# Gate and up in seven block products instead of eight, in a two-layer trunk on one core

## The chip, the cores and the metric

The kernel runs on one core of a Trainium2 chip, in one launch. The metric is the device time of that core in microseconds (us), the median over several executions of the program. Five engines work side by side, each through its own queue of instructions and in order: TensorE (PE, with its weight loads shown apart as PEld), VectorE (DVE), ScalarE (ACT), GpSimd (POOL) and SyncE (SP), which here issues most DMAs. An instruction that needs another engine's result waits at the head of its queue, and what stands behind it waits too.

## The reference

Two layers over 512 tokens of 1024 features. Each layer is a mixer and a feed-forward network (FFN), each inside a sandwich of norms:

```
for layer in range(2):
    x = x + rmsnorm(mixer(rmsnorm(x, mix_pre_g)), mix_post_g)
    x = x + rmsnorm(swiglu(rmsnorm(x, ffn_pre_g)), ffn_post_g)

def swiglu(h, w_gate, w_up, w_down):     # [512, 1024], two of [1024, 2816], [2816, 1024]
    return (silu(h @ w_gate) * (h @ w_up)) @ w_down
```

The mixer of layer 0 is forgetting attention (8 heads) beside causal pooling, that of layer 1 a gated linear recurrence. All is float32. The change concerns `h @ w_gate` and `h @ w_up`, and what makes and uses their operands.

## The kernel before

**Products.** A float32 operand a is held as two parts, ah and al, and a product is ah·bh + ah·bl + al·bh, three matmuls into the same bank of PSUM (`mm3`, L124 to L126). Weights come in units of 128 x 1024: SP loads a unit into one of 3 `raw` tiles (L142), ScalarE casts it to the high part (`whi`, L143), and VectorE subtracts to get the low part (`wlo`). VectorE's instructions are issued through a helper, so most of them bear its line, L89. `whi` and `wlo` have 4 buffers each. `unit()` hands out the next unit and issues the loads and splits of the two behind it, with high priority.

**Order.** Instructions are put into the program in the order of the code, each on its engine's queue; a scheduler that knows priorities may move some forward. Work for TensorE that needs results of other engines is put back by hand: `later(delay, fn)` queues it behind so many us of matmuls as counted by `tick`, and `need(...)` calls what is left of it up to the token blocks named.

**The end of a mixer.** `TokenMajor` makes the output projection of each block of 128 tokens; `Finish` then makes, per token block, the post-norm (two Squares on ScalarE L573, a product with the gain on VectorE, a power on GpSimd L553), the residual sum (`xres`), the next pre-norm (Square L590, power, `tmp<-xres,small,gain`), the transposes on TensorE (L610), and the split of the transposed activations into hTh (ScalarE, L613) and hTl (VectorE). The steps of one block follow each other from engine to engine. Blocks 2 and 3 come last, while the FFN already begins.

**The FFN.** 22 tiles of 128 gate columns and 22 of up columns, each the product of a unit with all 512 tokens over 8 slices of k: 24 matmuls. The first four tiles run in halves of 256 columns (`split_proj`), first over token blocks 0 and 1 in all four, then over 2 and 3, so that TensorE works while blocks 2 and 3 are still being normalised. The other 40 tiles are matmuls of 512 columns (`proj`) that read hTh and hTl as four pieces of 128. A pair's gate tile goes through Silu (L706), VectorE multiplies with the up tile (`tmp<-tmp,ps`), ScalarE casts the high part (`gT`, L709) and GpSimd subtracts the low part (L710). The down projection takes 22 units: 16 for all blocks, then the last 6 block by block, each block followed by its `Finish`.

**The start.** The first projection takes 8 steps k (`vs`, values and gates), each with one load of x and weights (L216 to L219) and matmuls of 264 and 256 columns. A load of constants (`in_sh`, L241) and three loads of weights follow; the constants' casts on VectorE (`idb`, `maskb`) stand in the queue between steps of this projection.

Of the kernel before, what the change touches and what calls it, by code (L numbers as in the profile page):

```python
# [15 lines left out]
P = 128  # L16
D = 1024
# [4 lines left out]
FT = FF // P  # L22
EPS = 1e-6
# [3 lines left out]
# columns of the packed per-partition constants and parameters  # L27
# [23 lines left out]
# shape constants: identity | causal mask | zeros, upper triangle with the diagonal, ones  # L51
# [7 lines left out]
def tile_trunk(ctx: ExitStack, tc: tile.TileContext, cst_d, sh_d, xw_d, x_d, gains_d, pw_d, w_d, out_d):  # L59
    """Every float32 product a.b is carried as ah.bh + ah.bl + al.bh on float32r,  # L60
    where ah holds the top 12 bits of a and al = a - ah the rest, exactly."""
# [17 lines left out]
    class Recorded:  # L79
        """an engine that remembers the last instruction given to it"""  # L80
# [21 lines left out]
    # work for the tensor engine that is queued behind `delay` us of other work of it,  # L102
    # while what it needs is being made
# [19 lines left out]
    def mm3(out, ah, al, bh, bl, start, stop, us=0.65):  # L123
        nc.tensor.matmul(out, lhsT=ah, rhs=bh, start=start, stop=False)  # L124
        nc.tensor.matmul(out, lhsT=ah, rhs=bl, start=False, stop=False)  # L125
        nc.tensor.matmul(out, lhsT=al, rhs=bh, start=False, stop=stop)  # L126
        tick(us)

# [4 lines left out]
    NU = w_d.shape[0]  # L133
# [5 lines left out]
    def split_weights(src, n, hi, lo):  # L139
        raw = pw.tile([P, D], F32, name="raw", tag="raw", bufs=3)  # L140
        with tc.high_priority():
            nc.sync.dma_start(out=raw[:, :n], in_=src)  # L142
            nc.scalar.copy(out=hi, in_=raw[:, :n])  # L143
            vec.tensor_sub(out=lo, in0=raw[:, :n], in1=f32(hi))

    def prefetch(n):
        while state["loaded"] < min(NU, state["used"] + n):
            hi, lo = place.get(state["loaded"], whl)()
            split_weights(w_d[state["loaded"]], D, hi, lo)
            ready.append((hi, lo))  # L150
            state["loaded"] += 1

# [27 lines left out]
    # the tensor engine's clock rises while the first loads are under way  # L180
# [9 lines left out]
    def log1p(out, e, u, d):  # L190
        """out = log(1 + e) for 0 <= e <= 1, with what the rounding of 1 + e takes off; u and d are scratch."""
# [7 lines left out]
    # ================= layer 0 mixer =================  # L199
# [4 lines left out]
    # values and forget gates, k outermost, on x*g; the row scale is applied on the way out.  # L204
    # columns: even heads, gates | odd heads
# [4 lines left out]
    for k in range(KT):  # L210
        xw = pw.tile([P, T + 520], F32, name="raw", tag="raw", bufs=3)
# [36 lines left out]
    # row scale of the first norm  # L248
# [41 lines left out]
    # -8 softplus(-lam)  # L290
# [4 lines left out]
    # c = cumsum(log f), as rows 32*b + 4*h + r for every b and r, by a product with the triangle  # L295
# [10 lines left out]
    def gates():  # L306
# [591 lines left out]
```

## Time and profile before

| | us |
|---|---|
| median of 3 runs | 1098.68 (1098.46 to 1099.26) |
| the profiled execution, first to last instruction | 1097.0 |
| TensorE busy in it | 1079.5 (98%) |
| VectorE busy | 485.1 (44%) |
| ScalarE busy | 421.3 (38%) |
| GpSimd busy | 139.7 (13%) |
| gate and up, layer 0 (189.32 to 437.10) | 247.8 |
| gate and up, layer 1 (721.65 to 969.51) | 247.9 |

The profile is of one execution, and its times count from the first instruction. "Busy" is the time in which at least one instruction of the engine ran. Matmuls overlap: the duration of one is longer than the distance between two starts, and what a matmul costs is read from the starts.

### The profile page before, as it was taken

How to read it: one execution, taken by the hardware profiler on the slowest of the kernel's cores; microseconds unless marked ns; L12 is line 12 of the kernel's file. 1: busy time of each engine (PE TensorE's matmuls, PEld its weight loads, DVE VectorE, ACT ScalarE, POOL GpSimd, SP SyncE). 2: the span in 40 equal slices, each digit the busy share in tenths (PEclk: the TensorE clock that was granted, in tenths of full speed). 3: DMA queues.
4: the chain of work that ended last, by engine and by line, in shares of the span. 5: the costliest groups of instructions: out<-in, count | busy, mean ns of one | idle time of the engine just before them, and what ended most of it. 6: DMA issues, size and time to landing. Idle time of an engine off the chain costs nothing.

```text
span 1097.0 us, 12987 instructions
## 1 busy us (share of the span) xinstructions
PE 1079.5 (98%) x5166; PEld 893.5 (81%) x5166; DVE 485.1 (44%) x665; ACT 421.3 (38%) x659; POOL 139.7 (13%) x140
## 2 busy tenths in 40 slices
PE   8999999999999999999999999999999999999997
PEld 7878787988888888888898887898888888888885
DVE  4899856522222222224348598543222222222323
ACT  6767634422222222114235984433222222221211
POOL 0020201111111111000003104101111111110000
PEclk9999999999999999999999999999999999999999
DMA  8644343322222222226113223313222222223401
GB/s 287 179 112 106 97 155 114 115 95 90 90 93 95 96 96 96 96 96 193 57 39 116 96 86 106 116 40 130 89 92 94 96 96 96 96 81 111 135 24 72
DMA packets 33292, 114.37 MB, mean 104 GB/s; under 512 B 4048, under 2 KB 4048, under 8 KB 33232
## 3 DMA queue, kind: packets, MB, share of 16 engines
q1 hardware_dynamic: 32656, 111.45, 31.1%
q10 hardware_dynamic: 576, 2.10, 0.5%
q8 instruction: 40, 0.66, 0.2%
q14 instruction: 20, 0.16, 0.0%
HBM read 107.24 MB, written 2.10 MB: 100 GB/s over the span
## 4 chain that ended last, share of the span: by engine, by line
PE 83%; DVE 8%; ACT 3%; issue 2%; DMA 2%; POOL 0%; SPq 0%; DVEq 0%; POOLq 0%; ACTq 0%
PE ps L125 27%; PE ps L124 27%; PE ps L126 27%; DVE wlo L89 2%; DVE tmp L89 2%; DVE cr L89 2%; DVE th L89 1%; ACT whi L143 1%; PE ps L610 1%; DMA tmp<-in_sh 1%; PE ps L475 1%; PE ps L495 1%; ACT th L774 1%; PE ps L447 0%; DMA raw<-in_xw 0%
## 5 line engine op out<-in xcount | busy, mean ns | idle before, releaser
L124 PE MATMUL ps<-hTh,whi 128*128 128x512 f32 (+1 forms) x1024 | 382.8, 375 | 0.2 <-DVE vs L89 0.2
L125 PE MATMUL ps<-hTl,whi 128*128 128x512 f32 (+1 forms) x1024 | 382.4, 374 | 0.0
L126 PE MATMUL ps<-hTh,wlo 128*128 128x512 f32 (+1 forms) x1024 | 382.4, 374 | 0.0
L143 ACT CAST whi<-raw 128x1024 fp32r<-128x1024 f32 x160 | 167.6, 1048 | 471.5 <-issue 176.2
L89 DVE TENSOR_TENSOR wlo<-raw,whi 128x1024 fp32r<-128x1024 f32 (+1 forms) x168 | 204.3, 1216 | 321.5 <-ACT whi L143 315.8
L126 PEld LDWEIGHTS ps<-hTh,wlo 128*128 128x128 f32 x1024 | 192.9, 188 | 36.6
L125 PEld LDWEIGHTS ps<-hTl,whi 128*128 128x128 f32 x1024 | 192.9, 188 | 36.3 <-issue 0.2
L124 PEld LDWEIGHTS ps<-hTh,whi 128*128 128x128 f32 x1024 | 192.5, 188 | 36.6 <-PE ps L126 0.4
L710 POOL TENSOR_TENSOR gT<-tmp,gT 128x512 fp32r<-128x512 f32 x44 | 78.4, 1781 | 407.1 <-ACT gT L709 407.1
L126 PE MATMUL ps<-whi,gT 128*128 128x512 f32 x256 | 99.6, 389 | 0.0
L124 PE MATMUL ps<-whi,gT 128*128 128x512 f32 x256 | 99.6, 389 | 0.0
L125 PE MATMUL ps<-wlo,gT 128*128 128x512 f32 x256 | 99.6, 389 | 0.0
L89 DVE TENSOR_TENSOR tmp<-tmp,ps 128x512 f32<-128x512 f32 x44 | 30.3, 688 | 144.0 <-PE ps L126 142.6
L553 POOL TENSOR_TENSOR small<-small,nhalf 128x1 f32<-128x1 f32 x28 | 15.4, 551 | 331.0 <-DVE small L89 328.4
L126 PEld LDWEIGHTS ps<-whi,gT 128*128 128x128 f32 x256 | 48.1, 188 | 10.1
L125 PEld LDWEIGHTS ps<-wlo,gT 128*128 128x128 f32 x256 | 48.1, 188 | 10.0
L124 PEld LDWEIGHTS ps<-whi,gT 128*128 128x128 f32 x256 | 48.1, 188 | 10.0
L89 DVE TENSOR_TENSOR tmp<-ps,gain 128x512 f32<-128x512 f32 x32 | 21.9, 690 | 55.5 <-ACT junk L573 55.4
L573 ACT ACTIVATE junk<-ps 128x512 bf16<-128x512 f32 x32 | 19.0, 596 | 62.0 <-PE ps L126 61.7
L124 PE MATMUL ps<-gT 128*128 128x512 f32 x96 | 37.5, 391 | 0.0
L126 PE MATMUL ps<-gT 128*128 128x512 f32 x96 | 37.4, 389 | 0.0
L125 PE MATMUL ps<-gT 128*128 128x512 f32 x96 | 37.4, 389 | 0.0
(179 smaller groups left out, 1108.3 us busy)
## 6 DMA issues: line engine op xcount, KB each, us to landing
raw<-in_w SPq DMA_DIRECT2D x180, 512.0 KB, 3.5
gain<-in_gains SPq DMA_DIRECT2D x7, 512.0 KB, 3.5
raw<-in_xw SPq DMA_DIRECT2D x6, 516.0 KB, 6.3
big<-in_x ACTq DMA_DIRECT2D x4, 512.0 KB, 6.9
big<-big SPq DMA_DIRECT2D x16, 128.0 KB, 2.6
xres<-in_x SPq DMA_DIRECT2D x4, 512.0 KB, 4.7
out_dram<-xres SPq DMA_DIRECT2D x3, 512.0 KB, 2.6
big<-tmp SPq DMA_DIRECT2D x8, 128.0 KB, 3.1
```

The lines of the kernel that those rows point to most:

```text
L89: self.last = fn(*a, **k)
L124: nc.tensor.matmul(out, lhsT=ah, rhs=bh, start=start, stop=False)
L125: nc.tensor.matmul(out, lhsT=ah, rhs=bl, start=False, stop=False)
L126: nc.tensor.matmul(out, lhsT=al, rhs=bh, start=False, stop=stop)
L143: nc.scalar.copy(out=hi, in_=raw[:, :n])
L475: nc.tensor.transpose(tp[:, b * P:(b + 1) * P], pr[i][:, j * P:(j + 1) * P], ident)
L495: nc.tensor.matmul(acc[:, dst], lhsT=v, rhs=parts[g][q][:, src], start=j == 0 and q == 0, stop=j == 3 and q == 1)
L553: nc.gpsimd.tensor_tensor(out=r, in0=ms, in1=nhalf[:, :1], op=ALU.pow)
L573: nc.scalar.activation(out=junk[:, cs], in_=acc, func=AF.Square, scale=1.0 / 32, accum_out=ss[:, hf:hf + 1])
L610: nc.tensor.transpose(tp[:, b * P:(b + 1) * P], h[:, k * P:(k + 1) * P], ident)
L710: nc.gpsimd.tensor_sub(out=v[:, 1], in0=g, in1=f32(v[:, 0]))
L774: tanhs.append(nc.scalar.activation(out=th[m], in_=ra[m], func=AF.Tanh, scale=coef[:, m:m + 1]))
```

## The change

**Blocks.** In gate and up the product h·W is cut into 2 x 2 blocks: h by its halves of tokens (blocks 0, 1 and blocks 2, 3) and of k, and W, for each pair j of gate and up tiles (256 columns each), by its halves of k and of columns. Seven block products replace eight, by Strassen's scheme in Winograd's form. There are 11 pairs j, and each of the seven products is 24 matmuls of 256 columns. The sums of activations that it needs (S1 to S4, beside the plain A11, A12 and A22) are made once per layer, on VectorE, when token blocks 2 and 3 are transposed (`Blocks.put`); they lie in hTh, hTl and two more tiles, `up`. The sums of weights (`raw<-raw`) are made for each j on VectorE before the split, and the sums of products (`y`, and `z`, `c` in `hx`) on VectorE after the matmuls. VectorE's helper now has line L100, the casts of weights L158, the transposes L743.

**The first five pairs.** A11 and A12 need blocks 0 and 1 alone. For j = 0 to 4 (LEAD) these two products run ahead, before the need for blocks 2 and 3, and their two weight quarters are loaded a second time for the sums. From j = 5 all seven products of a j come together, in the order A11, S1, S2, A12, S3, S4, A22.

**Down.** It stays 22 units with 512-column matmuls. Its activations are kept in float32 (`g`), and `part()` splits them on ScalarE and VectorE up to two units ahead of their use, into the places of hTh, hTl and `up`; GpSimd's subtractions are gone.

**Else.** There are 6 `raw` tiles instead of 3; the loads of weights in front of down's last steps go 8 units ahead instead of 10; units are laid out in another order in memory.

```diff
+LEAD = 5
+RAW = 6
+    def gate_recipes(first):
+        for j in range(LEAD):
+            recipes.append(lambda j=j: load(j, 0))
+            recipes.append(lambda j=j: load(j, 3))
+        for j in range(NP):
...
+            def q5(j=j, st=st):
+                if j < LEAD:
+                    p1(j, st)
+                st["12"] = load(j, 1)
+                add_to(st["v"], st["12"], vec)
+                return st["v"]
...
+            recipes.extend([q5, p6, p7, lambda st=st: st["22"], q4] if j < LEAD
+                           else [p1, q5, p6, p2, p7, lambda st=st: st["22"], q4])
+    class Blocks:
+        def put(self, i, tps):
...
+            def split(f, src):
+                hi, lo = (view(a)[:, :, cs] for a in slot(f))
+                nc.scalar.copy(out=hi, in_=src)
+                vec.tensor_sub(out=lo, in0=src, in1=f32(hi))
...
+            if i < 2:
+                for f, x, src in ((A11, x11, tv[0]), (A12, x12, tv[1])):
+                    split(f, src)
+                    nc.scalar.copy(out=x, in_=src)
+                return
+            ta, tb = tmp(), tmp()
+            x22, s1, s2, s3 = view(ta[:, :T]), view(ta[:, T:]), view(tb[:, :T]), view(tb[:, T:])
+            nc.scalar.copy(out=x22, in_=tv[1])
+            vec.tensor_sub(out=s1, in0=tv[0], in1=x22)
+            split(S1, s1)
+            vec.tensor_sub(out=s2, in0=s1, in1=x11)
+            split(S2, s2)
+            vec.tensor_sub(out=s3, in0=x11, in1=tv[0])
+            split(S3, s3)
+            vec.tensor_add(out=s1, in0=s2, in1=x12)
+            split(S4, s1)
+            split(A22, x22)
-        pre = split_proj(4)
-        for m in range(FT):
...
-            nc.gpsimd.tensor_sub(out=v[:, 1], in0=g, in1=f32(v[:, 0]))
+        def gate_product(bank, w, f, more=False):
+            for g in range(2):
+                for k in range(4):
...
+                    mm3(bank[:, g * 256:g * 256 + 256], wh[:, cs], wl[:, cs], fh[:, ts], fl[:, ts],
+                        not more and g == 0 and k == 0, g == 1 and k == 3, 0.356, more)
...
+        need(0, 1)
+        for j in range(LEAD):
+            led.append(first(j))
+            second(j, led[j][0])
+        need(2, 3)
+        for j in range(NP):
+            b1, y = led[j] if j < LEAD else first(j)
+            z, c = hx[:, j % 2, :T], hx[:, j % 2, T:]
+            b3 = ps()
+            gate_product(b3, unit(), S1)
+            b2 = ps()
+            gate_product(b2, unit(), S2)
+            vec.tensor_add(out=y, in0=b2, in1=y)
+            vec.tensor_sub(out=z, in0=b3, in1=y)
+            if j >= LEAD:
+                second(j, b1)
+            b4 = ps()
+            gate_product(b4, unit(), S3)
+            vec.tensor_sub(out=c, in0=z, in1=b4)
+            gated(j, 3, c, c[:, :256])
+            b5 = ps()
+            gate_product(b5, unit(), S4)
+            vec.tensor_add(out=z, in0=b5, in1=z)
+            gated(j, 2, z, z[:, :256])
+            gate_product(b4, unit(), A22, True)
+            vec.tensor_add(out=y, in0=b4, in1=y)
+            gated(j, 1, y, y[:, :256])
+        def part(k, ahead=2):
+            while len(parts) < min(FT, k + 1 + ahead):
...
+                nc.scalar.copy(out=hi, in_=src)
+                vec.tensor_sub(out=lo, in0=src, in1=f32(hi))
-        prefetch(tail + 4)
+        prefetch(TAIL + 2)
```

**Three places in the order of the instructions.** First VectorE, at the norm of blocks 2 and 3 at the end of layer 0's mixer. `xres<-tmp,small,xres` is the residual sum, of block 2 in one instruction and of block 3 in two, `tmp<-xres,small,gain` the normalised rows. Before:

```order
L89 SCALAR_TENSOR_TENSOR xres<-tmp,small,xres 128x1024
L89 TENSOR_SCALAR small<-small 128x1
L89 TENSOR_TENSOR tmp<-ps,gain 128x512
L89 SCALAR_TENSOR_TENSOR tmp<-xres,small,gain 128x512 x2
L89 TENSOR_TENSOR tmp<-ps,gain 128x512
L89 SCALAR_TENSOR_TENSOR small<-small 128x1
L89 SCALAR_TENSOR_TENSOR xres<-tmp,small,xres 128x512 x2
L89 TENSOR_TENSOR hTl<-ps,hTh 128x512
L89 SCALAR_TENSOR_TENSOR small<-small 128x1
L89 SCALAR_TENSOR_TENSOR tmp<-xres,small,gain 128x512 x2
```

The same place afterwards:

```order
L100 SCALAR_TENSOR_TENSOR xres<-tmp,small,xres 128x1024
L100 TENSOR_SCALAR small<-small 128x1
L100 TENSOR_TENSOR tmp<-ps,gain 128x512
L100 SCALAR_TENSOR_TENSOR tmp<-xres,small,gain 128x512
L100 TENSOR_TENSOR wlo<-raw,whi 128x1024
L100 SCALAR_TENSOR_TENSOR tmp<-xres,small,gain 128x512
L100 TENSOR_TENSOR tmp<-ps,gain 128x512
L100 SCALAR_TENSOR_TENSOR small<-small 128x1
L100 SCALAR_TENSOR_TENSOR xres<-tmp,small,xres 128x512 x2
L100 TENSOR_TENSOR wlo<-raw,whi 128x1024 x2
L100 SCALAR_TENSOR_TENSOR small<-small 128x1
L100 SCALAR_TENSOR_TENSOR tmp<-xres,small,gain 128x512 x2
```

Three splits of 1024 now stand between the normalised rows of block 2 and those of block 3. One subtraction of 512 for hTl no longer stands there.

On TensorE the transposes of block 3 (two groups of four, the first of each with its wait) stand in the products of the first units. Before:

```order
L124 MATMUL ps<-hTh,whi 128x256
L125 MATMUL ps<-hTl,whi 128x256
L126 MATMUL ps<-hTh,wlo 128x256
L610 MATMUL ps<-ident,tmp 128x128 [waits DVE_49]
L610 MATMUL ps<-ident,tmp 128x128 x3
L610 MATMUL ps<-ident,tmp 128x128 [waits DVE_49]
L610 MATMUL ps<-ident,tmp 128x128 x3
L124 MATMUL ps<-hTh,whi 128x256
```

and afterwards:

```order
L743 MATMUL ps<-ident,tmp 128x128 [waits DVE_49]
L743 MATMUL ps<-ident,tmp 128x128 x3
L137 MATMUL ps<-hTl,whi 128x256
L138 MATMUL ps<-hTh,wlo 128x256
L136 MATMUL ps<-hTh,whi 128x256
L137 MATMUL ps<-hTl,whi 128x256
L138 MATMUL ps<-hTh,wlo 128x256
L743 MATMUL ps<-ident,tmp 128x128 [waits DVE_49,PE_49]
L743 MATMUL ps<-ident,tmp 128x128 x3
L743 MATMUL ps<-ident,tmp 128x128 [waits DVE_49,PE_49]
L743 MATMUL ps<-ident,tmp 128x128 x3
L136 MATMUL ps<-hTh,whi 128x256 [waits Activation_49]
```

Block 3's transposes stood behind 90 matmuls of 256 columns; now 72 stand ahead of them, and the last group of block 2's (the first two rows) lies five matmuls earlier.

Second, VectorE in a pair j from 5 on, where `y<-ps,y` and `hx<-ps,y` take up the products S2 and S1, and `raw<-raw` are sums of weights. Before, a pair of tiles had there:

```order
L89 TENSOR_TENSOR tmp<-tmp,ps 128x512
L89 TENSOR_TENSOR wlo<-raw,whi 128x1024 x2
L89 TENSOR_TENSOR tmp<-tmp,ps 128x512
L89 TENSOR_TENSOR wlo<-raw,whi 128x1024 x2
L89 TENSOR_TENSOR tmp<-tmp,ps 128x512
```

and afterwards, from the first of these sums:

```order
L100 TENSOR_TENSOR y<-ps,y 128x512
L100 TENSOR_TENSOR hx<-ps,y 128x512
L100 TENSOR_TENSOR wlo<-raw,whi 128x1024 x2
L100 TENSOR_TENSOR g<-tmp,ps 128x256
L100 TENSOR_TENSOR raw<-raw 128x1024
L100 TENSOR_TENSOR hx<-hx,ps 128x512
L100 TENSOR_TENSOR raw<-raw 128x1024
L100 TENSOR_TENSOR wlo<-raw,whi 128x1024
L100 TENSOR_TENSOR g<-hx 128x256
L100 TENSOR_TENSOR raw<-raw 128x1024
L100 TENSOR_TENSOR hx<-ps,hx 128x512
L100 TENSOR_TENSOR y<-ps,y 128x512
```

Where a pair of tiles had two splits and one product, a pair j has 7 splits, 4 sums of weights, 5 sums of products and 4 products in all.

Third, the loads at the start of SP's queue. `in_xw` are the loads of the first projection, `in_sh` the constants, `in_w` and `in_pw` weights. Before:

```order
L217 DMA raw<-in_xw 128x520
L219 DMA raw<-in_xw 128x1032 x3
L241 DMA tmp<-in_sh 128x896
L219 DMA raw<-in_xw 128x1032 x3
L142 DMA raw<-in_w 128x1024 x2
L142 DMA raw<-in_pw 128x512
```

and afterwards:

```order
L299 DMA raw<-in_xw 128x520
L301 DMA raw<-in_xw 128x1032 x6
L153 DMA raw<-in_pw 128x512
L153 DMA raw<-in_w 128x1024
L323 DMA tmp<-in_sh 128x896
L153 DMA raw<-in_w 128x1024 x10
```

The load of the constants stood behind three large loads; it stands behind six, and two of weights.

## Rows read from the trace of the kernel before

**Rows 1.** The whole core: span and mean granted clock of TensorE.

```profile
core 0: 1097.0 us, clock 0.997
```

**Rows 2.** The page's first part: busy us, share and instructions of each engine.

```profile
PE 1079.5 (98%) x5166; PEld 893.5 (81%) x5166; DVE 485.1 (44%) x665; ACT 421.3 (38%) x659; POOL 139.7 (13%) x140
```

**Rows 3.** The page's second part: busy tenths in 40 equal slices.

```profile
PE   8999999999999999999999999999999999999997
...
DVE  4899856522222222224348598543222222222323
```

**Rows 4.** Stretches: PE, PEld, DVE, ACT, POOL busy, granted clock, DMA share, GB/s.

```profile
189.32:214.01 24.69, 24.69 (x209) 24.57 (x208) 14.00 (x21) 11.92 (x21) 4.00 (x5) 1.00 0.25 87
214.01:437.10 223.09, 223.09 (x962) 180.88 (x961) 62.78 (x60) 62.87 (x80) 35.63 (x20) 1.00 0.29 97
437.10:524.19 87.09, 87.09 (x385) 72.07 (x384) 27.41 (x23) 23.44 (x23) 1.77 (x1) 1.00 0.41 130
721.65:746.43 24.78, 24.78 (x210) 24.67 (x208) 12.76 (x19) 10.32 (x19) 3.47 (x4) 1.00 0.19 65
746.43:969.51 223.08, 223.08 (x963) 180.87 (x961) 62.77 (x60) 62.93 (x80) 35.55 (x20) 1.00 0.29 97
```

**Rows 5.** TensorE's timeline: start, duration, engine, line, operation, tile; matmuls of 256 columns.

```profile
25.82 0.28 PE L124 MATMUL ps<-whi,hTh 128*128 128x264 f32 x1
...
31.46 0.28 PE L126 MATMUL ps<-whi,hTl 128*128 128x256 f32 x1
...
189.32 0.28 PE L124 MATMUL ps<-hTh,whi 128*128 128x256 f32 x1
...
195.71 1.04 PE L610 MATMUL ps<-ident,tmp 128*128 128x128 f32 x8
196.51 0.37 PE L124 MATMUL ps<-hTh,whi 128*128 128x256 f32 x1
```

**Rows 6.** VectorE's timeline: single instructions, and rows of equal ones (x2, x4).

```profile
31.34 1.65 DVE L89 SCALAR_TENSOR_TENSOR vs<-ps,small,vs 128x256 fp32r<-128x256 f32 x4
...
186.82 1.28 DVE L89 TENSOR_TENSOR tmp<-ps,gain 128x512 f32<-128x512 f32 x2
...
705.99 1.22 DVE L89 TENSOR_TENSOR wlo<-raw,whi 128x1024 fp32r<-128x1024 f32 x1
707.12 0.74 DVE L89 SCALAR_TENSOR_TENSOR tmp<-xres,small,gain 128x512 f32<-128x512 f32 x1
707.79 0.68 DVE L89 TENSOR_TENSOR hTl<-ps,hTh 128x512 fp32r<-128x512 f32 x1
```

**Rows 7.** The page's fifth part: count, busy, mean ns of one, idle before.

```profile
L143 ACT CAST whi<-raw 128x1024 fp32r<-128x1024 f32 x160 | 167.6, 1048 | 471.5 <-issue 176.2
...
L89 DVE TENSOR_TENSOR tmp<-tmp,ps 128x512 f32<-128x512 f32 x44 | 30.3, 688 | 144.0 <-PE ps L126 142.6
```

**Rows 8.** VectorE's timeline at the norms of blocks 2 and 3, layer 0.

```profile
190.09 1.28 DVE L89 SCALAR_TENSOR_TENSOR xres<-tmp,small,xres 128x1024 f32<-128x1024 f32 x1 [0.73 <-POOL small L553]
192.65 0.15 DVE L89 TENSOR_SCALAR small<-small 128x1 f32<-128x1 f32 x1 [1.28 <-ACT junk L590]
...
199.87 1.41 DVE L89 SCALAR_TENSOR_TENSOR tmp<-xres,small,gain 128x512 f32<-128x512 f32 x2 [0.67 <-POOL small L553]
```

**Rows 9.** VectorE's timeline at the norm of block 2, layer 1.

```profile
726.14 1.42 DVE L89 SCALAR_TENSOR_TENSOR tmp<-xres,small,gain 128x512 f32<-128x512 f32 x2 [0.66 <-POOL small L553]
```

**Rows 10.** Stretches, columns as in Rows 4: a pause of TensorE and the 4 us after.

```profile
680.00:684.00 4.00, 2.46 (x10) 1.48 (x10) 2.59 (x3) 3.39 (x5) 1.28 (x1) 1.00 0.72 213
684.00:688.00 4.00, 4.00 (x12) 3.17 (x11) 2.34 (x3) 2.25 (x3) 1.65 (x1) 0.57 0.80 275
```

**Rows 11.** The chain of waits at the start: start, us, what.

```profile
9.21 9.06 DMA tmp<-in_sh
```

**Rows 12.** VectorE's timeline at the landing of the constants.

```profile
18.29 0.23 DVE L89 CAST idb<-tmp 128x128 bf16<-128x128 f32 x1 [5.86 <-DMA tmp<-in_sh]
```

**Rows 13.** The first 30 us, columns as in Rows 4.

```profile
0.00:30.00 30.00, 25.36 (x187) 22.68 (x188) 14.15 (x28) 19.12 (x32) 2.55 (x8) 1.00 0.77 272
```

More of the change, by code (lines that the diff above doesn't have):

```diff
@@ L121, in need, with mm3 @@
             pending.pop(0)[1]()
[L123 to L126, printed above, removed]
+    def mm3(out, ah, al, bh, bl, start, stop, us=0.65, more=False):
+        nc.tensor.matmul(out, lhsT=ah, rhs=bh, start=start, stop=False, skip_group_check=more)
+        nc.tensor.matmul(out, lhsT=ah, rhs=bl, start=False, stop=False, skip_group_check=more)
+        nc.tensor.matmul(out, lhsT=al, rhs=bh, start=False, stop=stop, skip_group_check=more)
         tick(us)
@@ L132, in tile_trunk @@
     place = {}
-    NU = w_d.shape[0]
     def whl():
@@ L146, in prefetch, with split_weights, add_to @@
+    def split_weights(raw, hi, lo):
+        with tc.high_priority():
+            nc.scalar.copy(out=hi, in_=raw)
+            vec.tensor_sub(out=lo, in0=raw, in1=f32(hi))
+    def add_to(acc, other, eng):
+        with tc.high_priority():
+            eng.tensor_add(out=acc, in0=acc, in1=other)
+    recipes = []
     def prefetch(n):
-        while state["loaded"] < min(NU, state["used"] + n):
+        while state["loaded"] < min(len(recipes), state["used"] + n):
             hi, lo = place.get(state["loaded"], whl)()
-            split_weights(w_d[state["loaded"]], D, hi, lo)
+            raw = recipes[state["loaded"]]()
+            w = raw.shape[-1]
+            split_weights(raw, hi[:, :w], lo[:, :w])
@@ L150, in prefetch, with plain, load, p1 @@
             ready.append((hi, lo))
             state["loaded"] += 1
+    def plain(first, n):
+        for u in range(first, first + n):
+            recipes.append(lambda u=u: rawtile(w_d[u]))
+    def gate_recipes(first):
+        def load(j, q):
+            return rawtile(w_d[first + 4 * j + q])
+        for j in range(LEAD):
+            recipes.append(lambda j=j: load(j, 0))
+            recipes.append(lambda j=j: load(j, 3))
+        for j in range(NP):
+            st = {}
+            def p1(j=j, st=st):
+                st["v"] = load(j, 0)
+                return st["v"]
[4 more added lines that the diff above has]
+                add_to(st["v"], st["12"], vec)
+                return st["v"]
+            def p6(j=j, st=st):
+                st["22"] = load(j, 2)
+                add_to(st["v"], st["22"], vec)
+                return st["v"]
+            def p2(j=j, st=st):
+                st["21"] = load(j, 3)
+                return st["21"]
+            def p7(j=j, st=st):
+                add_to(st["12"], st["22"], vec)
+                return st["12"]
+            def q4(j=j, st=st):
+                if j < LEAD:
+                    p2(j, st)
+                add_to(st["v"], st["21"], vec)
+                return st["v"]
+            recipes.extend([q5, p6, p7, lambda st=st: st["22"], q4] if j < LEAD
+                           else [p1, q5, p6, p2, p7, lambda st=st: st["22"], q4])
@@ L566, in __init__, with half @@
             self.u = {}
-        def half(self, i, hf, acc):
-            if hf == 0:
+        def half(self, i, hf, acc, made_by=None):
+            if i not in self.u:
                 self.u[i] = (small(2), tmp())
@@ L618, in block @@
             later(T3, second)
+    n0 = KT + 4 + KT
+    plain(0, n0)
+    gate_recipes(n0)
+    n1 = n0 + 2 * FT
+    plain(n1, FT + KT + 4 + KT + KT)
+    n1 += FT + 3 * KT + 4
+    gate_recipes(n1)
+    plain(n1 + 2 * FT, FT)
     stacks = []
@@ new lines, in first, with second @@
+        def first(j):
+            b1 = ps()
+            gate_product(b1, unit(), A11)
+            y = gs[NP - 1 - j][:, 1] if j < LEAD else ytile()
+            nc.scalar.copy(out=y, in_=b1)
+            return b1, y
+        def second(j, b1):
+            gate_product(b1, unit(), A12, True)
+            gated(j, 0, b1, tmp()[:, :256])
+        led = []
+        need(0, 1)
[3 more added lines that the diff above has]
+        need(2, 3)
@@ L716, in ffn @@
+        for n in range(4):
+            place[state["used"] + FT - TAIL + n] = lambda: tuple(gt(F32R).rearrange("p a t -> p (a t)") for _ in range(2))
+        tm = TokenMajor([lambda k=k: part(k) for k in range(FT)], TAIL)
         tm.lead(range(3), (0, 1))
         tm.lead(range(3), (2, 3))
-        tm.lead(range(3, FT - tail), range(NB))
-        fin = Finish(1 if layer == 0 else 3)
-        prefetch(tail + 4)
+        tm.lead(range(3, FT - TAIL), range(NB))
+        fin = Finish(1 if layer == 0 else 3, Plain())
```

115 lines of the change are left out of this document (76 added, 39 removed).

## The prediction

> **What bounds the kernel now.** I read the whole-core answer first: one execution of 1097.0 us at full clock [rows 1]. The median of the runs is 1098.68, so some 1.7 us lie outside the span; the sum below is made against this execution and 1.7 is added back. The page's first part comes next: matmuls fill 1079.5 us, 98% [rows 2], and by the slices they do so in all of the middle, while VectorE stands at two tenths through the long flat stretches [rows 3]. So outside the first and last slices a us taken from TensorE is a us of the kernel, until another engine is late. The table of stretches gives the stage that changes [rows 4]: gate and up of layer 0 take 24.69 + 223.09 = 247.8 us, those of layer 1 24.78 + 223.08 = 247.9, with TensorE busy in each of these us, VectorE in 77 of 248 in layer 0 (14.00 + 62.78).
>
> **TensorE's part.** Before, a layer has 44 tiles of 24 matmuls, 4 of them in halves of 256 columns. Afterwards 11 pairs j of seven products of 24 matmuls, 1848 of 256 columns: seven eighths of the columns, in instructions half as wide. The price of a 256 is in the trace: 54 start between 189.32 and 195.71, 0.1183 each [rows 5]; the 192 of the split stretch take 24.69 less two groups of transposes (0.80 the first, by the starts at 195.71 and 196.51; with 0.9 for the second), 0.1197 each. These read two blocks of 128 columns, the new ones 256 in a row; matmuls of 264 and 256 columns that read in a row start every 0.120 (47 steps from 25.82 to 31.46 [rows 5]). I take 0.1185: 1848 x 0.1185 = 219.0, with the transposes 220.7, 27.1 us less per layer, 54.3 in both. Ends: 0.120 costs 2.8 a layer; half of a 512 read in a row (87.09 / 384 = 0.2268 [rows 4]), 0.1134, gives 9.4 more.
>
> That a 256 comes every 0.118 with weights of its own is two things at once in the row: loads fill 24.57 of 24.69 us beside matmuls that fill all of it [rows 4]. The Trainium skill ("TensorE: Matmul & The Clock Gate", section "The mechanism") says that a load runs beside matmuls under way only when its row group differs; here all rows are used, and the trace differs from that sentence. By it load and matmul would take turns, which is the fifth rival.
>
> **VectorE's part.** Back to back, one 1024-wide difference takes 1.13 (705.99 to 707.12); of two 512s in 1.28 the second adds 0.60 to the 0.68 that one alone takes; four 256s take 1.65 in their nearest row, 0.41 each [rows 6]. For a 256 I use 0.33 for the plain two-operand form, estimated as 0.60 less 256 columns of (1.13 - 0.60) / 512. For j from 5 on VectorE has 7 splits and 4 sums of 1024, 5 sums of 512 and 4 products of 256: 11 x 1.13 + 5 x 0.60 + 4 x 0.33 = 16.8, TensorE 7 x 24 x 0.1185 = 19.9. It is covered, and the order has the splits up to four units ahead. For j under 5, whose two first products went ahead, it is 9 x 1.13 + 3.0 + 1.0 = 14.2 against 14.2: no margin. ScalarE (7 casts of about 0.95 start to start, 1.05 long [rows 7], four Silu) has half of that and is not late. GpSimd loses its 44 differences of 512, worth nothing.
>
> **Where it is late: the start of gate and up.** Up to the norm of block 2, VectorE's order is that of before, so I start from 190.09 [rows 8]. New on VectorE in front of block 3's normalised rows are three splits (3.4), which partly fill the waits on GpSimd; done by hand with the rows' durations, ScalarE's Square in 192.65 and the casts, h of block 3 comes at 203.4 instead of 199.87, its first half at 204.1. TensorE's order has only three products (72 x 0.1185 = 8.5) and block 2's transposes in front of block 3's: it arrives at 198.7 and stands 5.4 us. From 204.7 VectorE has until the second split of j = 0 one 256, 9 of 1024 and 16 of 512: 0.3 + 10.2 + 9.6 = 20.1, so 224.8. That product (S2) is the ninth and would end at 189.3 + 9 x 2.844 + 1.7 = 216.6; it ends at 227.6. Layer 0 loses 11.0.
>
> Layer 1: block 2's rows are normalised at 726.14 as before [rows 9]. From there to the same split stand 4 x 0.66, 12 x 1.13, 18 x 0.60, two of 256, and 0.8 of small things and waiting: 28.5, so 754.7. S2 is the tenth there and would end at 721.65 + 28.4 + 1.7 = 751.8; it ends at 757.5. Layer 1 loses 5.7.
>
> After an idle TensorE the clock can fall: with matmuls in 2.46 of the 4 us from 680, the granted clock was 0.57 of 2.4 GHz, mostly the 1.2 level, in the next four [rows 10]. Twelve matmuls there took what eight take: about 1.7 us. I put 1.7 in each layer, 3.4 (0 to 7). For j under 5, where no margin is, 1 a layer (0 to 4).
>
> **The rest.** The split of the down operands adds 0.60 on VectorE and one 512 cast on ScalarE to a unit of 5.4 us that has 1.13 and 0.95: hidden; bare it would be 13 a layer. Six raw tiles instead of three bring the first loads forward, but the load of the constants now goes behind six large loads, two weight loads and x. It landed at 18.3 (9.21 + 9.06 [rows 11]), and the casts that VectorE holds behind it, and with them the fifth k, waited for it [rows 12]. 7.5 MB now come before its end, at 272 GB/s [rows 13] 27.6 us; it then holds up the seventh k. By that TensorE ends this stage at some 34 instead of 31.5, with a faster stream at about its old time. I take +2 (-1 to 4). Of the next mixer's four first units two are split only when down ends, some 2 us after it each; the third is wanted 5.7 us after: nothing.
>
> **Sum.** 1097.0 - 54.3 + 11.0 + 5.7 + 3.4 + 2 + 2 = 1066.8, with the 1.7 outside 1068.5.
>
> **Rivals.**
> First, TensorE never waits: the queues run further ahead than I read. All 54.3 are kept: 1098.7 - 54.3 + 2 = 1046. For it: VectorE is idle most of the stage. Against: the order, in which block 3's transposes stand after three products. 12%.
> Second, VectorE is the bound of the whole first half of the stage: with a wait on another engine before most instructions nothing overlaps its neighbour and each costs its full 1.22 or 0.69 [rows 6, 7], a 256 0.42 by the same estimate. A j under 5 is then 9 x 1.22 + 5 x 0.69 + 3 x 0.42 = 15.7, 1.5 more, 15 in both layers, and the two starts some 5 more: 1088. For it: no margin in those five. Against: waits that have long been met cost nothing in the rows. 20%.
> Third, slower: the round trip of each sum (sum on VectorE, cast on ScalarE, difference on VectorE) stays bare in an in-order queue. A j costs 4 x (1.22 + 1.05 + 1.22) + 3 x (1.05 + 1.22) + 3.4 + 1.7 = 25.9, where 248 / 11 = 22.5 stood: 37 a layer, 1175. It decides once more than 22.5 - 16.8 = 5.7 of the 9.1 us of exposed casts are bare. Against: the order puts other work between a sum and its difference nearly everywhere. 6%.
> Fourth, a 256 costs half a 512: 18.8 less, 1050. The Trainium skill (same page, "Back-to-back issue gap") gives N / 2.4 + 2.5 ns for a lone matmul, 109 for 256; by that it would be 202 a layer, 34 less in both. The trace's 0.118 speaks against it. 4%.
> Fifth, load and matmul in turns: 0.188 (180.88 / 961 [rows 4]) + 0.1185 is 0.307 each, 348 a layer more, near 1,795. The rows exclude it almost wholly: 1%.
>
> **How the numbers follow.** The forecast has 57%: 1068. 1044 to 1090 holds it with the first, second and fourth. Repeats lie within 0.1% of each other, so 0.2% (2.2 us) is what can be told from no change. Faster: 57 + 12 + 20 + 4, a little off, 92%; slower 7%; the same 1%.
>
> **What would show it.** Right: 256s every 0.1185 in all of gate and up; stretches of about 233 and 228 us there; in layer 0 a stand of some 5 us before the last transposes, then two shorter ones before the first S1 and S2 products; from j = 5 no gaps. VectorE at 16 to 17 us of work in 20. Wrong: gaps on TensorE that recur with each j, each released by a VectorE split (second or third rival), or none at all (first).

## The result: faster by about 1%, little more than a third of the forecast, and the profile after

The changed kernel takes 1087.43 us (median of 4 runs, 1083.38 to 1087.84) against 1098.97 (median of 4): 11.5 us less, where the forecast's sum had 30.2 for the profiled span. The ratio over all runs is 0.9883, with a 95% interval of 0.9862 to 0.9903. The profiled execution spans 1085.6 us. Its busy times and slices answer to [rows 2, 3]:

```profile
PE 1041.1 (96%) x6558; PEld 931.0 (86%) x6558; DVE 768.8 (71%) x1045; ACT 516.9 (48%) x815; POOL 60.7 (6%) x96
...
PE   8989999789999999999999999897999999999997
```

TensorE's busy time fell by 38.4 us and the span by only 11.4: the rest is idle time that was not there. The stretches, with the columns of [rows 4], say where:

```profile
0.00:33.58 33.58, 27.50 (x201) 24.30 (x201) 16.56 (x29) 20.73 (x34) 2.91 (x8) 1.00 0.82 312
33.58:196.74 163.16, 156.20 (x759) 124.59 (x760) 124.78 (x257) 96.57 (x199) 19.06 (x40) 0.98 0.44 122
196.74:434.01 237.27, 225.76 (x1865) 223.65 (x1864) 210.88 (x258) 116.90 (x169) 2.19 (x4) 0.99 0.38 120
434.01:557.51 123.50, 123.50 (x547) 100.82 (x545) 49.86 (x62) 36.98 (x55) 3.29 (x6) 1.00 0.30 94
557.51:670.83 113.32, 113.32 (x593) 96.22 (x592) 85.81 (x101) 75.97 (x110) 16.12 (x19) 1.00 0.36 116
670.83:722.67 51.84, 47.83 (x209) 38.73 (x208) 28.41 (x35) 24.51 (x45) 13.29 (x12) 0.97 0.24 72
722.67:957.08 234.41, 225.16 (x1865) 223.76 (x1864) 209.74 (x256) 115.48 (x165) 1.65 (x3) 0.99 0.38 119
957.08:1085.57 128.49, 121.81 (x530) 98.96 (x528) 42.76 (x51) 29.78 (x44) 2.20 (x4) 0.99 0.22 75
```

Against the same stretches of the kernel before:

| stretch | before | after | change | forecast |
|---|---|---|---|---|
| start and mixer 0 | 189.3 | 196.7 | +7.4 | +2 |
| gate and up, layer 0 | 247.8 | 237.3 | -10.5 | -13.4 |
| down 0 and what follows | 121.6 | 123.5 | +1.9 | 0 |
| mixer 1 up to its output projection | 113.7 | 113.3 | -0.4 | 0 |
| output projection of mixer 1 | 49.3 | 51.8 | +2.6 | 0 |
| gate and up, layer 1 | 247.9 | 234.4 | -13.4 | -18.8 |
| down 1 and the end | 127.5 | 128.5 | +1.0 | 0 |
| sum | 1097.0 | 1085.6 | -11.4 | -30.2 |

Two of these stretches carry much of what follows. In the kernel before, mixer 0 without its first stage and the output projection of mixer 1 read:

```profile
31.96:189.32 157.36, 153.82 (x759) 123.19 (x760) 126.24 (x255) 94.68 (x193) 20.84 (x40) 1.00 0.43 128
672.39:721.65 49.26, 47.72 (x209) 38.72 (x208) 29.56 (x36) 24.32 (x41) 10.25 (x10) 0.97 0.35 117
```

One execution is not exact here. In the profiled executions of e3, e4, e6 and e7 below, which leave mixer 0 as it is in the changed kernel, gate and up begin at 193.44, 193.69, 194.01 and 196.68: the first row of the table is a loss of 4 to 7 us.

Once a layer is under way it runs as forecast. One pair j in the flat part, and below it the product after the first stand:

```profile
354.23:374.17 19.94, 19.94 (x170) 19.94 (x169) 17.27 (x21) 8.94 (x13) 0.00 (x0) 1.00 0.32 106
213.45:217.68 4.23, 4.23 (x26) 4.23 (x25) 4.23 (x7) 1.11 (x2) 0.00 (x0) 0.65 0.40 155
```

The pair's 168 matmuls start every 0.1187 us (19.94 / 168; forecast 0.1185), VectorE has 17.27 of work in 19.94 (forecast 16.8 of 19.9), and TensorE stands nowhere. The lower row is a product of 24 matmuls that takes 4.23 instead of 2.85, at a granted clock of 0.65 of 2.4 GHz, between its two levels on average, after the 4.94 us of standing in the next rows. These are all of TensorE's waits from block 3's transposes to the second product of j = 0:

```profile
211.86 1.94 PE L743 MATMUL ps<-ident,tmp 128*128 128x128 f32 x8 [4.94 <-DVE tmp L100]
227.32 0.39 PE L136 MATMUL ps<-hTh,whi 128*128 128x256 f32 x1 [1.08 <-ACT whi L158]
228.58 0.39 PE L138 MATMUL ps<-hTh,wlo 128*128 128x256 f32 x1 [0.75 <-DVE wlo L100]
232.48 0.38 PE L136 MATMUL ps<-hTh,whi 128*128 128x256 f32 x1 [1.07 <-ACT whi L158]
233.79 0.39 PE L138 MATMUL ps<-hTh,wlo 128*128 128x256 f32 x1 [0.81 <-DVE wlo L100]
```

The stand of 5 us before the transposes was forecast at 5.4. The later rows are S1 and S2, each held by its cast and then by its split.

ScalarE's rows show what these two casts waited for, by the profile:

```profile
226.22 1.04 ACT L158 CAST whi<-raw 128x1024 fp32r<-128x1024 f32 x1 [0.65 <-PE ps L137]
231.39 1.04 ACT L158 CAST whi<-raw 128x1024 fp32r<-128x1024 f32 x1 [3.33 <-PE ps L137]
```

Each starts as TensorE ends a product, the second as S1 ends. In the compiled order the ten products ahead do not all come before S1 and S2, as the section on the change has it: A12 of j = 2, 3 and 4 stands behind S1, two of the three behind S2 in layer 1 and all three in layer 0. Their split weights hold three of the four `whi` and `wlo` tiles, and S1 and S2 both use the fourth. So in layer 0 a cast and a split lie bare in front of each of the two. VectorE is nearly always busy there (13.3 us of the 13.9 from the transposes to S1, all of the 9.1 from there to the end of S2), so its chain and the tiles bind together; more tiles were not tried.

### The profile page after: what moved, and what is told of

It reads as the page before. It is cut to its first block, busy times and chain, and to the rows that moved or that the text cites. A ratio compares the mean times of both kernels' runs of the same rounds, so it can differ in the third digit from the quotient of the medians.

```text
span 1085.6 us, 16315 instructions
## 1 busy us (share of the span) xinstructions
PE 1041.1 (96%) x6558; PEld 931.0 (86%) x6558; DVE 768.8 (71%) x1045; ACT 516.9 (48%) x815; POOL 60.7 (6%) x96
## 5 line engine op out<-in xcount | busy, mean ns | idle before, releaser
L158 ACT CAST whi<-raw 128x1024 fp32r<-128x1024 f32 x230 | 239.0, 1047 | 310.4 <-PE ps L137 113.1
L100 DVE TENSOR_TENSOR wlo<-raw,whi 128x1024 fp32r<-128x1024 f32 (+1 forms) x238 | 286.3, 1212 | 124.7 <-ACT whi L158 119.6
L136 PE MATMUL ps<-hTh,whi 128*128 128x256 f32 (+1 forms) x960 | 294.6, 307 | 5.5 <-ACT whi L158 2.5
L138 PE MATMUL ps<-hTh,wlo 128*128 128x256 f32 (+1 forms) x960 | 294.0, 307 | 3.8 <-DVE wlo L100 3.8
L137 PE MATMUL ps<-hTl,whi 128*128 128x256 f32 (+1 forms) x960 | 292.2, 305 | 3.5 <-DVE hTl L100 3.5
L138 PEld LDWEIGHTS ps<-hTh,wlo 128*128 128x128 f32 x960 | 182.4, 190 | 13.3 <-DVE wlo L100 4.6
L136 PE MATMUL ps<-up,whi 128*128 128x256 f32 x528 | 149.8, 284 | 2.2 <-DVE hx L100 2.1
L137 PE MATMUL ps<-up,whi 128*128 128x256 f32 x528 | 149.4, 283 | 0.0
L138 PE MATMUL ps<-up,wlo 128*128 128x256 f32 x528 | 149.2, 283 | 0.0
L100 DVE TENSOR_TENSOR raw<-raw 128x1024 f32<-128x1024 f32 x88 | 106.9, 1220 | 8.1 <-DMA raw<-in_w 7.8
L136 PEld LDWEIGHTS ps<-up,whi 128*128 128x128 f32 x528 | 101.1, 191 | 3.1 <-DVE hx L100 3.0
L137 PEld LDWEIGHTS ps<-up,whi 128*128 128x128 f32 x528 | 101.2, 192 | 0.0
L138 PEld LDWEIGHTS ps<-up,wlo 128*128 128x128 f32 x528 | 101.1, 192 | 0.0
L100 DVE TENSOR_TENSOR tmp<-ps,gain 128x512 f32<-128x512 f32 x32 | 21.9, 690 | 59.0 <-ACT junk L705 58.9
```

Source lines behind the costliest of these rows:

```text
L100: self.last = fn(*a, **k)
L158: nc.scalar.copy(out=hi, in_=raw)
```

## The experiments

Ratios and intervals are against the kernel before, run on the same chip in the same job. Theory A to G and the rivals are those of the expectations. The scheduler gives each variant an order of its own on TensorE: in layer 0, S2 ends as the 9th product of the stage in the changed kernel and in e5, as the 10th in e7, the 11th in e4, the 12th in e9 and e10 and the 16th in e6. These runs change that order beside what they are named for.

**Six raw tiles.** In the kernel before, here and for the loads of the first projection; to make room, the program's scratch for DMAs shrinks to that of the changed kernel (`dynamic_dma_scratch_size=1024`, part of the change too):

```
-        raw = pw.tile([P, D], F32, name="raw", tag="raw", bufs=3)
+        raw = pw.tile([P, D], F32, name="raw", tag="raw", bufs=6)
...
```

> The kernel before with six raw tiles instead of three (and the smaller scratch that makes room for them), nothing else. Theory A: the six tiles let weight loads stand ahead of the constants and of the moves of the attention in SyncE's queue, and that made mixer 0 7.4 us longer in the changed kernel: 1104 to 1107 here, with the start of gate and up at 195 to 197 instead of 189.3. Rival: the loss in mixer 0 comes from something else in the change, and more tiles cost nothing: 1098 to 1100, gate and up from 189 to 190.

Measured: 1108.38, ratio 1.0086 (1.0072 to 1.0099), slower. Mixer 0 and the output projection of mixer 1:

```profile
34.86:196.82 161.96, 156.43 (x758) 124.85 (x759) 124.95 (x257) 95.02 (x196) 20.24 (x40) 0.98 0.42 121
680.14:732.90 52.76, 48.76 (x210) 39.40 (x208) 28.40 (x35) 22.34 (x41) 13.29 (x12) 0.94 0.23 71
```

Gate and up begin at 196.82 instead of 189.32, and the output projection takes 52.76 instead of 49.26. Both places pay, 7.5 and 3.5 us, with none of the block products there; the profiled execution is the slowest of six (1104.94 to 1110.16). So the six tiles, or the smaller scratch that goes with them, cost what theory A says and somewhat more.

**Three raw tiles in mixer 0 alone, and in both mixers.** In the changed kernel the other three tiles come from a second ring that only the FFNs use:

```
+        tag = "raw" if state["loaded"] < n0 or state["raw"] % 2 else "rawb"
-        raw = pw.tile([P, D], F32, name="raw", tag="raw", bufs=RAW)
+        raw = pw.tile([P, D], F32, name="raw", tag=tag, bufs=3)
...
+            order(dma, state["dma"])
...
```

The line with `order` keeps the loads in the order of the code, which was not tried apart. The smaller scratch stays, and the second run treats mixer 1 in the same way.

> The changed kernel, with only three raw tiles in use up to the end of layer 0's mixer and six afterwards. Theory A: mixer 0 gets back 5.5 to 7.4 us, the rest stays: 1080 to 1082, gate and up of layer 0 from 189.3 to 191. Rival: no change, 1087, gate and up from 196.7.

> The changed kernel, with only three raw tiles in use in both mixers and six in the FFNs. Theory A (loads that run ahead push other work back): beside the some 7 us of mixer 0 also the 2.5 us that the output projection of mixer 1 is longer than before (51.8 against 49.3): 1080 to 1082, that stretch 49 to 50. Rival: that stretch comes from the changed kernel's other order: 1083, 51.8.

Measured: 1083.17, ratio 0.9864 (0.9847 to 0.9880), with gate and up from 189.82 and an output projection of mixer 1 that stays at 51.73; and 1078.37, ratio 0.9812 (0.9798 to 0.9825). The stretches of the second:

```profile
32.38:190.43 158.05, 153.76 (x759) 123.17 (x759) 127.41 (x250) 95.83 (x196) 22.50 (x40) 1.00 0.46 140
...
665.46:714.44 48.98, 46.70 (x209) 37.46 (x208) 29.68 (x36) 26.60 (x45) 10.34 (x10) 1.00 0.45 150
```

Both losses go with the ring, while the smaller scratch stays: mixer 0 gets its 5 us back (163.16 to 158.05), the output projection its 2.9 (51.84 to 48.98). So it is the tiles. How it comes about in mixer 0 is read from SyncE's queue. Before, six loads of weights and then the moves of the attention:

```profile
29.43 15.06 SPq L142 DMA_DIRECT2D raw<-in_w  x6
44.54 1.16 SPq L375 DMA_DIRECT2D big<-big  x2
```

and in the changed kernel nine, from 20.19 to 48.28; then its longest wait in this stretch (total, times, longest) and the two waits of TensorE that follow:

```profile
20.19 28.09 SPq L153 DMA_DIRECT2D raw<-in_w  x9
48.34 1.16 SPq L457 DMA_DIRECT2D big<-big  x2
```

```profile
SPq L153 <- DVE lr L100: 10.9, 1, 10.9
```

```profile
60.21 0.88 PE L529 MATMUL ps<-big 128*128 128x256 f32 x4 [1.83 <-DMA big<-tmp]
...
64.29 0.55 PE L530 MATMUL ps<-big 128*128 128x256 f32 x1 [2.73 <-issue]
```

More loads fit, so more are queued ahead of the moves; one of them waits 10.9 us, by the profile until VectorE comes past `lr` (the gates), and the moves stand behind it. They are issued 3.8 us later and the scores that read them wait (what ended the second wait, the profile does not name). The other traces agree: in e1 the moves start at 49.63, with the same two waits of 1.26 and 2.55; in e5 they start at 45.83, and 0.2 us of the first wait is left and nothing of the second. Which of the nine loads did it was not tried apart. In the output projection of mixer 1 it is something else: SyncE's queue holds nothing but loads of weights there, and TensorE's wait for one cast of weights is 2.6 us in the changed kernel and in e1, 0.5 in the kernel before and in e5. How six tiles make that cast late stays open.

**Sums of weights on GpSimd for the first five pairs.** The first of four such edits, one for each sum:

```
-                add_to(st["v"], st["12"], vec)
+                add_to(st["v"], st["12"], nc.gpsimd if j < LEAD else vec)
...
```

> The changed kernel with the sums of weights of the first five pairs on GpSimd instead of VectorE (20 of 44 a layer). Theory B: VectorE's chain from block 3's normalised rows to the second split of j = 0 sets the stands of TensorE at the start of gate and up; four to five sums of 1.13 leave it, so about 4 us a layer: 1078 to 1082. Rival C: TensorE is held there by ScalarE's casts and the loads, and nothing moves: 1086 to 1088. Rival D: a sum of 1024 takes GpSimd some 3.5 us (twice the 1.78 of its 512 before), the splits come later by more than VectorE saves: 1090 to 1097.

Measured: 1120.25, ratio 1.0204 (1.0185 to 1.0222). Rival D's way, and worse than it said: gate and up take 253.31 and 254.03, 16.0 and 19.6 us more. GpSimd and VectorE at the same time:

```profile
209.54 5.18 POOL L163 TENSOR_TENSOR raw<-raw 128x1024 f32<-128x1024 f32 x2 [1.91 <-DMA raw<-in_w]
```

```profile
210.53 1.94 DVE L100 TENSOR_TENSOR tmp<-tmp,hx 128x512 f32<-128x512 f32 x1
212.39 2.89 DVE L100 TENSOR_TENSOR hTl<-tmp,hTh 128x512 fp32r<-128x512 f32 x1
215.21 0.68 DVE L100 TENSOR_TENSOR up<-tmp,up 128x512 fp32r<-128x512 f32 x1
```

A difference of 512 that takes 0.68 takes 2.89 beside the second of GpSimd's sums of 2.6 us, and ends just after it; the one before takes 1.94 beside the first. In these rows two sums on GpSimd, 2.6 us each where VectorE itself needs 1.13, hold VectorE up by 1.3 and 2.2 us. The Trainium skill ("GPSIMD Engine Reference", section "Specifications") says that GpSimd shares its interfaces to the on-chip memory with VectorE and contends with VectorE's instructions that read two inputs from there; the trace agrees. Rival D's late splits are in the rows too: from 228.58 on VectorE stands 7.18 us for a cast of weights, and GpSimd makes the next two sums from 227.72 to 232.83.

**All sums of weights left out.** The 88 calls of `add_to` are dropped.

> The changed kernel with all 88 sums of weights left out (the products use the unsummed quarters). Theory B: the stands at the starts fall from 16.2 and 13.3 us a layer to about 11 and 8, the waits from j = 5 on were none: 1075 to 1079. Rival: VectorE is the bound in the whole first half, all stands go: 1058 to 1064. Rival C (ScalarE and loads): 1086 to 1088.

Measured: 1076.30, ratio 0.9797 (0.9784 to 0.9809). Gate and up:

```profile
193.69:427.41 233.72, 225.78 (x1866) 224.51 (x1864) 167.34 (x216) 117.35 (x169) 2.19 (x4) 0.99 0.38 122
717.26:945.09 227.83, 223.81 (x1866) 222.82 (x1864) 166.35 (x214) 115.19 (x165) 1.65 (x3) 0.99 0.39 123
```

They are 3.6 and 6.6 us shorter; of 43 us a layer that VectorE no longer works, only these count. Theory B's sizes were 5 a layer; the rivals' were all of the stands (16 and 13) and 0.

**Seven pairs ahead instead of five.** `LEAD = 7`; the stored first products of j = 5 and 6 are then overwritten by later results, so this part of the computation is changed.

> The changed kernel with seven pairs whose A11 and A12 run ahead instead of five. Theory B (VectorE's chain up to the second split of j = 0 sets the stands, while TensorE works off what runs ahead): 4 more products give TensorE 11.4 us of work for 4 more splits (4.5 us) on VectorE, so the stands lose 4 to 7 us a layer: 1074 to 1080. Rival E: seven of the eight banks of PSUM are then held by these products, and the products S1 and S2 wait for banks: 1088 to 1095.

Measured: 1091.27, ratio 0.9926 (0.9914 to 0.9939), 3.8 slower than the changed kernel. Gate and up 240.87 and 236.50: theory B's number fails here. Rival E's range, 1088 to 1095, holds the time, and the run does not settle it: TensorE's longest wait in gate and up of layer 1 (3.0 us) ends with the copy of a first product out of its bank (`g<-ps`), most of the others with casts and splits of weights, which still pass through four tiles. Why more work ahead brought nothing stays open.

**Block 3's transposes further back.** `T2 = 10.3` instead of 4.3.

> The changed kernel with the transposes of block 3 put further back (T2 10.3 instead of 4.3), behind four products instead of three. Theory B: VectorE's chain stays as long, only the clock's fall after the stand may go: stand before the transposes 2 instead of 4.9 in layer 0, what follows takes it back: 1085 to 1088. Rival F: the stand itself is the loss, 3 us a layer come back: 1080 to 1083.

Measured: 1084.20, ratio 0.9861 (0.9842 to 0.9881). TensorE's waits in layer 0, two short ones left out:

```profile
211.79 1.68 PE L743 MATMUL ps<-ident,tmp 128*128 128x128 f32 x8 [2.15 <-DVE tmp L100]
...
231.65 0.39 PE L136 MATMUL ps<-hTh,whi 128*128 128x256 f32 x1 [3.65 <-ACT hTh L660]
232.99 0.58 PE L137 MATMUL ps<-hTl,whi 128*128 128x256 f32 x1 [0.95 <-DVE hTl L100]
```

The 4.94 became 2.15, and 4.6 us came up later, for S1's operand: gate and up of layer 0 take 236.89 instead of 237.27, those of layer 1 232.36 instead of 234.41. In layer 0 the stand that was taken away came back, and rival F is out there; in layer 1 the 2 us lie between the two, as the total does (theory B had 1085 to 1088, rival F 1080 to 1083).

**What S1 and S2 read comes first on VectorE.** On top of the three raw tiles in both mixers, `Blocks.put` issues the rest behind block 3's S1 and S2. What is new, with the lines on where block 2's values lie cut:

```
...
+            def rest():
+                split(S3, s3)
+                vec.tensor_add(out=s1, in0=s2, in1=x12)
+                split(S4, s1)
+                split(A22, x22)
+            resting.append(rest)
+            if i == 3:
+                while resting:
+                    resting.pop(0)()
...
```

> Three raw tiles in the mixers (as e5), and on VectorE the parts of blocks 2 and 3 that the products S1 and S2 read come first: the split of S3, and the sums and splits of S4 and A22, of both blocks are issued behind S1 and S2 of block 3 (block 2's in-between values lie in free g tiles). Theory B (the chain of VectorE up to the second split of j = 0 sets the stands): some of the 9 instructions of 0.60 a layer that need not stand there leave it, up to 5 us a layer, so 1068 to 1075 against e5's 1078.4. Rival H: VectorE's total over the first five pairs decides, and what is put back holds S3 and S4 up as long: 1077 to 1080.

> As e9, and block 3's transposes put further back as in e7 (T2 10.3). Theory B: the stand before the transposes falls from 4.9 to 2 and comes back in front of S1, less what the clock's fall cost: 0 to 2 us less than e9. Rival F (the stand itself is the loss): 3 us a layer less than e9.

Measured: 1069.73, ratio 0.9739 (0.9721 to 0.9758), and with the later transposes 1070.67, ratio 0.9749 (0.9730 to 0.9767). Gate and up in e5, and then in the first of the two:

```profile
190.43:428.49 238.06, 228.31 (x1865) 226.26 (x1864) 210.72 (x258) 117.06 (x168) 2.20 (x4) 0.98 0.35 120
...
714.44:949.36 234.92, 225.77 (x1866) 224.16 (x1865) 209.38 (x256) 115.47 (x165) 1.65 (x3) 0.99 0.35 119
```

```profile
191.50:426.19 234.69, 227.45 (x1865) 225.42 (x1864) 210.57 (x258) 116.53 (x168) 2.19 (x4) 0.99 0.35 122
...
712.26:940.33 228.07, 223.69 (x1865) 222.38 (x1864) 209.00 (x256) 115.00 (x165) 1.65 (x3) 1.00 0.36 123
```

VectorE does the same work (210.57 and 209.00 us, 210.72 and 209.38 in e5), in another order, and the stage is 3.4 and 6.8 us shorter. Theory B's range holds the time and rival H is out. But TensorE's order changed with it: all ten products ahead now come in front of S2 in layer 0, where seven did in e5, and S2 is taken up 46.9 us after the start of the stage (at 238.40) instead of 41.8 (at 232.25). Which of the two orders made the gain is not shown. This is the fastest version here, by the medians 17.7 us under the changed kernel. Later transposes add nothing to it.

**Another place for hTh and hTl.** In the changed kernel, and then in the kernel before:

```
+    pa = pool("acts")
-    hh = pc.tile([P, KT * T], F32R, name="hTh")
+    hh = pa.tile([P, KT * T], F32R, name="hTh")
```

> The changed kernel with hTh and hTl in another place of the on-chip memory (from 109,376 bytes instead of 1,632), the weight tiles and the small ones below them. In the changed kernel's down projection a matmul of 512 columns starts every 233 ns where its activations lie in hTh or hTl and every 227 where they lie in up. Theory G: the place makes the 6 ns; they go, 1.9 us in each down projection, some 1.7 in mixer 1's input projection: 1081 to 1085. Rival: it is not the place, 233 stays: 1086 to 1088.

> The kernel before, with hTh and hTl in another place of the on-chip memory, as in e8 (from 104,160 bytes). Theory G (the place makes a matmul of 512 columns start every 232 to 233 ns instead of 227): 960 of gate and up in each layer read them, 5 us a layer, with mixer 1's 288 and mixer 0's some 13 us in all: 1084 to 1088. Rival: only operands that are loaded as weights are slowed so (e8's down projection), reading them as the moving operand costs 232 wherever they lie: 1095 to 1098.

Measured: 1086.26, ratio 0.9882 (0.9869 to 0.9896), and 1086.92, ratio 0.9895 (0.9878 to 0.9911). The same matmuls of the down projection of layer 0, by form (count, busy, mean ns), first in the changed kernel, then with the other place:

```profile
L138 PE MATMUL ps<-whi,hTh 128*128 128x512 f32 x48 | 19.0, 396 | 0.0
...
L138 PE MATMUL ps<-whi,up 128*128 128x512 f32 x48 | 18.7, 390 | 0.0
```

```profile
L139 PE MATMUL ps<-whi,hTh 128*128 128x512 f32 x48 | 18.7, 389 | 0.0
```

The 6 ns go with the place, in starts too (233 to 227 ns). Down 0 falls from 123.50 to 121.55, mixer 1 up to its output from 113.32 to 111.99. But gate and up rise, 237.27 to 240.06 and 234.41 to 236.93: the matmuls of 256 columns that read hTh and hTl start every 0.120 there instead of 0.118. So theory G is right on its stretches and its total is not. In the kernel before, where most of gate and up is matmuls of 512, it is a gain:

```profile
187.99:430.54 242.55, 242.55 (x1170) 205.02 (x1168) 76.80 (x81) 74.66 (x101) 39.87 (x25) 1.00 0.31 98
```

242.55 instead of 247.78, and 12.7 us in all. Here hTh and hTl are the operands that move through the array, in e8's down projection they are loaded as weights: both are slowed. The change of place alone is worth as much as the change of this case.

## Why the prediction was wrong

The sign and the range held; the size did not. Its sum had 1066.8 for the span, and 1085.6 came: 18.8 us, in three of its steps. That the range still holds the time is owed to the width of its rivals, not to the sum.

**"Six raw tiles instead of three ... I take +2."** Failed: the start and mixer 0 lost 7.4 (4 to 7 over several executions), the output projection of mixer 1, which the sum did not name for this, 2.6. The constants did land late, and the cast on VectorE waited for them, to answer [rows 12]:

```profile
25.06 0.23 DVE L100 CAST idb<-tmp 128x128 bf16<-128x128 f32 x1 [4.90 <-DMA tmp<-in_sh]
```

The first stage ended at 33.6, as forecast (34). The other 5.8 us lie behind it: I followed the loads only to the end of that stage and asked what they carry, not what stands behind them in SyncE's queue afterwards. That the six tiles cost this, e1, e2 and e5 show; the way through the queue is read from the traces of mixer 0, and for mixer 1 it is open.

**The stands at the start of gate and up: 22.1 forecast, 30.3 came** (237.3 and 234.4 less 220.7 each). In layer 0 the size of the chain on VectorE nearly holds: 20.1 from block 3's rows to the second split, 21.4 measured (212.29 to 233.66, where the next instruction starts), S2 over at 235.0 by the forecast moved by the later start, 236.46 measured. The 1.7 that the sum adds for the clock is not on top of that: the slow product of 4.23 us lies before a wait that VectorE and the weight tiles end anyway. Two small errors cancel there, by luck. What came on top are 4.2 us after S2, where 1 was put for j under 5, most of it four short waits. The forecast also took the splits to run "up to four units ahead" and did not ask which units hold the four tiles at S1 and S2. In layer 1 the step that failed is "0.8 of small things and waiting". Up to the second split VectorE waited more than that, for casts above all:

```profile
733.17 1.23 DVE L100 TENSOR_TENSOR wlo<-raw,whi 128x1024 fp32r<-128x1024 f32 x1 [1.32 <-ACT whi L158]
734.87 0.42 DVE L100 TENSOR_TENSOR g<-tmp,ps 128x256 f32<-128x256 f32 x1 [0.47 <-ACT tmp L857]
735.80 1.23 DVE L100 TENSOR_TENSOR wlo<-raw,whi 128x1024 fp32r<-128x1024 f32 x1 [0.52 <-ACT whi L158]
...
741.48 1.23 DVE L100 TENSOR_TENSOR raw<-raw 128x1024 f32<-128x1024 f32 x1 [0.91 <-DMA raw<-in_w]
...
759.96 1.23 DVE L100 TENSOR_TENSOR wlo<-raw,whi 128x1024 fp32r<-128x1024 f32 x1 [1.69 <-ACT whi L158]
```

That is 4.9 us, and S2 ended 6.0 after its forecast moved by the later start (764.5 against 758.5). But the path was not the forecast one. S1 stood for its own operand, hTl of block 3, and ran slowly after it; the last of the casts above waited for S1's end:

```profile
753.78 0.58 PE L137 MATMUL ps<-hTl,whi 128*128 128x256 f32 x1 [3.46 <-DVE hTl L100]
```

```profile
753.78:758.98 5.20, 5.20 (x24) 5.20 (x25) 4.49 (x8) 2.40 (x5) 0.00 (x0) 0.50 0.00 0
```

```profile
758.88 1.05 ACT L158 CAST whi<-raw 128x1024 fp32r<-128x1024 f32 x1 [2.21 <-PE ps L137]
```

From 753.78 to the end of S2 TensorE stands nowhere. So S1's operand came late, by the first four of VectorE's waits (3.2 us) among other things, and the clock, at 0.50, cost 2.35 us on the path (5.20 less 2.85; 1.7 was put for it, beside the 758.5). e4 shows that less work on VectorE shortens these starts, as the forecast's mechanism has it; its size was read from counts of work, with the waits between engines and the weight tiles left out. How the 8.2 us divide among these is read from the trace and was not tried by itself.

**The rest, put at nothing: 1.9 in down 0, and 1.0 in the last stretch.** The split beside down is hidden, as said: TensorE is busy in all of the 123.50. But the activations now lie in hTh and hTl, whose place makes each matmul 6 ns slower; 288 of them are 1.8 us. e8 shows it: down 0 falls by 1.95 there, the last stretch from 128.49 to 126.55. No row of before had these tiles as operands of the down projection; the 512s of gate and up in [rows 4] had the 232 in them, unremarked.

**Right:** the price of a matmul of 256 columns (0.1187 against 0.1185), VectorE's load in a pair, no stand from the middle of the stage on, 5 us of stand before the last transposes. That GpSimd's differences are worth nothing was not tried by itself.

**The rivals.** The second, VectorE as the bound with each instruction at its full length, named 1088, the time that came. Its mechanism did not: in the trace VectorE's instructions of 512 start 0.60 apart in this chain (216.47, 217.07, 217.67) and those of 1024 1.13 to 1.15, and 10 of the 18.8 us lie outside gate and up: that the number fits is luck. The third is far off in time, but its bare round trip of cast and split does occur, before S1 and S2 of j = 0 in layer 0. The first (never waits), fourth and fifth are out by the stands and by 0.1187. The fifth's 1,795 was also added up wrongly: its 348 a layer is the excess over the forecast price, so it belongs on 1068 and gives some 1765.

## What to carry to other kernels

A larger buffer for loads can change the order of everything else in the queue that issues them: list what stands behind the loads that can now go ahead, to the end of the kernel, and price those. When fewer matmuls are bought with sums on another engine, the flat part is easily paid and the first stage is not; there the order of the instructions was worth as much (10.2 us in e9) as all the sums of weights left out (10.1 in e4). Work put ahead does not help by itself: it also holds the tiles that the next product needs. A stand of the busy engine that is moved need not be gained: look at the chain behind it.

## What the runs showed of the hardware

Where an operand of TensorE lies in the on-chip memory changes the time of a matmul. 512 columns that use hTh and hTl start every 232 to 233 ns where the program lays these from byte 1,632 of a partition (changed kernel) or 16,992 (kernel before, whose scratch for DMAs is larger), and every 226 to 227 from 109,376 (e8) or 104,160 (e11). With 256 columns the place in the changed kernel is the faster one (117.8 against 120 ns in e8). No cause was found, and the weight tiles moved with them. In e3, VectorE's differences of two operands took longer beside a sum on GpSimd (0.68 became 1.94 and 2.89).
